# First query block of a sliding-window attention: no value product and no scores for the empty block in front of it

## The chip, the core and the metric

The kernel runs on one core of a Trainium2 chip. The metric is device time in microseconds (us) of one execution of the whole program, as the median of several runs. The profile is of one execution; its span goes from the first to the last instruction. The engines are named as the profile names them: PE for matmuls (TensorE), PEld for the loads of the stationary operand, DVE (VectorE), ACT (ScalarE), POOL (GpSimd), and SP for the queue that issues most transfers.

## The reference, cut to what matters

One inference step of a two-layer decoder, all in float32: a causal pooling mixer, then sliding-window attention with learned sinks. There are 1024 prompt positions and 8 single-token decode rows; the model width is 2048, with 32 query heads and 4 key/value heads of 64.

```
def banded_blocks(a):                       # each block of 128 keys with the block in front of it
    ax = jnp.concatenate([jnp.zeros_like(a[:, :WINDOW]), a], axis=1)
    ax = ax.reshape(B, nb + 1, WINDOW, *a.shape[2:])
    return jnp.concatenate([ax[:, :-1], ax[:, 1:]], axis=2)

s = jnp.einsum('...qkgd,...skd->...kgqs', q, k) * (HEAD_DIM ** -0.5)
mask = (kp <= qp) & (qp - kp < WINDOW) & (kp >= 0)
s = jnp.where(mask, s, NEG)
m = jnp.maximum(jnp.max(s, axis=-1, keepdims=True), sink)
p = jnp.exp(s - m)
p = p / (jnp.sum(p, axis=-1, keepdims=True) + jnp.exp(sink - m))
o = jnp.einsum('...kgqs,...skd->...qkgd', p, v)
```

Queries come in blocks of 128. Each block sees its own 128 keys and the 128 in front of them, of which the mask leaves the trailing 128 positions. The first block of the prompt has nothing in front of it: its front block is a block of zeros with positions below zero, and the mask (`kp >= 0`) leaves none of it.

## The kernel before

The prompt is worked on in two chunks: chunk c = 0 holds positions 0 to 511, chunk c = 1 positions 512 to 1023 and the decode rows. Each layer is an input projection and an output projection (`PHASES`: ai, ao for the first layer, bi, bo for the second), once per chunk. A projection in float32 precision is three matmuls for each piece of weights: high part by high part, high by low, low by high (L684 to L686 in the projections that use Strassen's seven products, L712 to L714 in the plain ones). The weights come by SP from memory, DVE adds or subtracts pieces of them (L349), ACT rounds them to the high part (L505), DVE forms the low part (L520).

The attention of a chunk is woven into its bi phases. It goes by 16 tiles t of two heads each; of a tile, head j sits on 64 of the 128 partitions. `attend(c, t, ...)` books the steps of one tile on later ticks of the projection: `product` puts a piece of PE work behind the weights of that tick, `at` a piece of other work. The steps of one tile, in order:

- `score` (L1878). For each of NB = 4 query blocks b, each head j and each quarter a of the block (32 queries, h = 32a), one float32 matmul with 64 rows of contraction and 32 columns of stationary operand. Its moving operand is the band of 160 keys that those 32 queries can see: from key h of the block in front to key h + 31 of the own block. Eight such matmuls (4 quarters, 2 heads) make a block, 32 a tile of heads. They write `self.S` (the program's pS) in PSUM, where a block has 256 columns: 128 for the front block's keys, 128 for its own.
- `select` and `largest` copy the front half out to SBUF with ACT (L1895) and put the own half over it with DVE where key <= query, so that 128 columns hold the whole window. In chunk 0 the front half of block 0 isn't read: POOL fills its place with -1e30 (L1893), and ACT copies blocks 1 to 3 alone.
- `expo`, `total` and `norm` (ACT, DVE) make the probabilities, `turn` (L1931, PE) transposes them, `keep` copies them to `w` (ACT) and, with those of own keys set to zero, to `wp` (DVE, L1941).
- `values` (L1955): for each block b, the own values times `w`, then the difference "front values minus own values" (`Vd`) times `wp`, added in PSUM; in each, head j is one float32 matmul with 128 rows and 64 columns of stationary operand and 128 moving columns. That is 4 matmuls a block, 16 a tile. In chunk 0, block 0, `wp` is all zeros, since no key of the front block has a probability.
- `gate` (L1964, DVE) multiplies with the gate, and the result goes to memory.

The keys lie in `kT` with 128 columns in front of the chunk's 512; in chunk 0 POOL sets these 128 to zero, in chunk 1 they are the last keys of chunk 0 (`kv_open`).

PE, DVE and ACT run in the order of the source: a function at the end of the build ties each instruction to the one before it on its engine. The instructions on SP and POOL are ordered by the scheduler of the language's library, which also sets all waits.

Of the kernel before, what the change touches and what calls it, by code (L numbers as in the profile page):

```python
# [16 lines left out]
P = 128  # L17
# [173 lines left out]
class Kern:  # L191
# [1670 lines left out]
    def attend(self, c, t, at, s1, s2, late=False, ticks=CLOSE):  # L1862
# [6 lines left out]
        x = {}  # L1869

        def score():
            s, q, lastq = self.qs.pop((c, t))
            for b in range(NB):
                for j in range(2):
                    r = slice(64 * j, 64 * j + 64)
                    for a in range(4):
                        h, k = 32 * a, b * P + 32 * a
                        nc.tensor.matmul(  # L1878
                            self.S[h : h + 32, j, b * 256 + h : b * 256 + h + 160], q[r, k : k + 32],
                            self.kT[t // 8][r, k : k + 160], start=True, stop=True,  # L1880
                        )
            if lastq:
                s.free()
# [63 lines left out]
        def values():  # L1947
            o = x["o"] = self.S[:, 1, :512] if late else self.psO()
            for b in range(NB):
                bs = slice(b * P, (b + 1) * P)  # L1950
                for n, (V, p) in enumerate(((self.V[b + 1], x["w"].a), (self.Vd[b], x["wp"].a))):
                    for j in range(2):
                        vs = slice((2 * (t // 8) + j) * HD, (2 * (t // 8) + j + 1) * HD)
                        ms = slice((2 * b + j) * P, (2 * b + j + 1) * P)
                        nc.tensor.matmul(  # L1955
                            o[64 * j : 64 * j + 64, bs], V[:, vs], p[:, ms], start=n == 0, stop=n == 1
                        )
            x["w"].free()
            x["wp"].free()

        def gate():
# [13 lines left out]
            if j == 1 or t == 15 or self.sg.get((c, t + 1), (None,))[0] is not z:  # L1975
                z.free()

        self.product(at, 2, score)
        for n, go in zip(ticks, (
            select, largest, lambda: expo(0), lambda: expo(1), total, lambda: norm(0), lambda: norm(1)  # L1980
        )):
            self.at(at + n, go)
        self.product(at + s1, 0, turn)
        self.at(at + s1 + 1, keep)
        self.product(at + s1 + s2, 1, values)
        self.at(at + s1 + s2 + 1, gate)

# [501 lines left out]
```

## Time and profile before

| | |
|---|---|
| runs | 2308.86, 2309.34 and 2309.92 us (median 2309.34) |
| span of the profiled execution | 2308.8 us, 50518 instructions; its own device time isn't listed apart from the span |
| granted TensorE clock | 0.999 over the span |
| scores (L1878) | 2048 records on PE in 32 places (16 tiles by 2 chunks), 64 x 32 stationary, 160 moving columns |
| values (L1955) | 1024 records on PE in 32 places, 128 x 64 stationary, 128 moving columns |
| those of chunk 0 | scores from 1148.1 to 1524.6 us, values from 1193.6 to 1558.6 us |

A matmul of two float32 operands leaves two records on PE and two on PEld, so a tile's 32 score matmuls are 64 records and its 16 value matmuls 32. Records overlap: a row's duration holds the time that the array takes to pass data through, and the pace at which work goes on is read from the starts of neighbouring records, not from durations. In a timeline, neighbouring records of one line are merged into one row with their count; a row of a very short stretch holds those that are open in it.

### The profile page before, as it was taken

Reading aid. Unit: us, or ns where it says so; the run is one execution under the profiler, and the core shown is the slowest. Engines: PE = TensorE matmul, PEld = TensorE weight load, DVE = VectorE, ACT = ScalarE, POOL = GpSimd, SP = SyncE. Lnnn points to the kernel's source line nnn. Section 1 sums busy time; section 2 is a strip of 40 time slices with the busy share of each in tenths; the row PEclk is TensorE's granted clock in tenths of the full one; section 3 lists DMA queues with packets and bytes.
Section 4 is the critical chain, followed back from the end, with each engine's and each line's share of the span. In section 5 each row is a group of like instructions: output and inputs, shape, how many; then the busy total and the mean of one; then the engine's idle time right before and its main releaser. Section 6 shows DMA issues by size and latency. Waiting matters only on the chain.

```text
span 2308.8 us, 50518 instructions
## 1 busy us (share of the span) xinstructions
PE 2286.2 (99%) x20417; PEld 2216.1 (96%) x20417; DVE 1943.5 (84%) x2415; ACT 1389.0 (60%) x2547; POOL 191.1 (8%) x359
## 2 busy tenths in 40 slices
PE   9999999999999999999999999999999999999998
PEld 7999999999999999999889999999999999999998
DVE  8888889877868878998878888999877777888997
ACT  5544446544546556555576766785776678656665
POOL 0111100010000000000001111100000000000001
PEclk9999999999999999999999999999999999999999
DMA  7879679988989989999767667777787778799894
GB/s 260 284 245 315 229 252 327 317 302 300 303 304 323 339 293 321 317 385 359 235 241 249 224 237 243 263 273 233 236 261 233 248 241 293 245 365 360 286 342 149
DMA packets 246395, 648.31 MB, mean 281 GB/s; under 512 B 25201, under 2 KB 106001, under 8 KB 246161
## 3 DMA queue, kind: packets, MB, share of 16 engines
q1 hardware_dynamic: 204288, 493.13, 63.7%
q0 software_dynamic: 41872, 151.96, 17.0%
q8 instruction: 159, 2.61, 0.5%
q14 instruction: 76, 0.61, 0.1%
HBM read 463.00 MB, written 172.47 MB: 275 GB/s over the span
## 4 chain that ended last, share of the span: by engine, by line
PE 56%; DVE 1%; DMA 1%; ACT 0%; issue 0%; POOL 0%; SPq 0%; DVEq 0%; POOLq 0%
PE pD L684 15%; PE pD L686 14%; PE pD L685 14%; PE pO L1955 2%; PE pD L712 2%; PE pD L714 2%; PE pD L713 2%; PE pS L1878 2%; PE pS L1931 1%; DMA m<-in_wob 0%; PE pS L1955 0%; PE pO L684 0%; PE pO L685 0%; PE pO L686 0%; DVE m L520 0%; DMA m<-in_wib 0%
## 5 line engine op out<-in xcount | busy, mean ns | idle before, releaser
L684 PE MATMUL pD<-m,m 128*128 128x260 f32 (+1 forms) x5088 | 1441.1, 283 | 4.4 <-ACT pD L623 2.2
L686 PE MATMUL pD<-m,m 128*128 128x260 f32 (+1 forms) x5088 | 1434.0, 282 | 5.8 <-DVE m L520 5.8
L685 PE MATMUL pD<-m,m 128*128 128x260 f32 (+1 forms) x5088 | 1434.2, 282 | 0.0
L684 PEld LDWEIGHTS pD<-m,m 128*128 128x128 f32 x5088 | 958.9, 188 | 13.7 <-issue 6.2
L686 PEld LDWEIGHTS pD<-m,m 128*128 128x128 f32 x5088 | 959.5, 189 | 7.6 <-DVE m L520 7.4
L685 PEld LDWEIGHTS pD<-m,m 128*128 128x128 f32 x5088 | 958.6, 188 | 0.5
L520 DVE TENSOR_TENSOR m<-m,m 128x1024 fp32r<-128x1024 f32 x690 | 834.1, 1219 | 94.4 <-ACT m L505 37.9
L505 ACT CAST m<-m 128x1024 fp32r<-128x1024 f32 x690 | 720.6, 1049 | 247.5 <-DVE m L349 122.4
L349 DVE TENSOR_TENSOR m<-m,m 128x1024 f32<-128x1024 f32 x136 | 166.2, 1222 | 8.6 <-DMA m<-in_wia 5.6
L847 DVE TENSOR_TENSOR m<-m,m 128x1024 fp32r<-128x1024 f32 (+1 forms) x118 | 144.0, 1225 | 7.4 <-ACT m L838 5.8
L838 ACT CAST m<-m 128x1024 fp32r<-128x1024 f32 (+1 forms) x118 | 123.3, 1051 | 8.3 <-DVE m L520 3.9
L657 ACT COPY m<-pD 128x260 f32<-128x260 f32 (+1 forms) x88 | 32.9, 374 | 125.8 <-PE pD L686 125.6
L645 DVE TENSOR_TENSOR m<-pD,m 128x260 f32<-128x260 f32 (+1 forms) x92 | 38.3, 417 | 74.3 <-ACT pD L644 68.2
L1914 ACT ACTIVATE m<-m,sm 128x128 f32<-128x128 f32 x256 | 99.4, 392 | 0.0
L623 ACT ACTIVATE pD<-pD 128x260 f32<-128x260 f32 (+1 forms) x90 | 33.3, 370 | 98.8 <-PE pD L686 98.4
L1181 PE MATMUL pD<-m,m 128*128 128x260 f32 (+1 forms) x528 | 91.5, 323 | 0.0
L712 PE MATMUL pD<-m,m 128*128 128x512 f32 x224 | 89.1, 398 | 0.0
L714 PE MATMUL pD<-m,m 128*128 128x512 f32 x224 | 88.2, 394 | 0.0
L713 PE MATMUL pD<-m,m 128*128 128x512 f32 x224 | 88.1, 393 | 0.0
L1181 PEld LDWEIGHTS pD<-m,m 128*128 128x128 f32 x528 | 79.4, 188 | 8.2
L1927 ACT ACTIVATE m<-m,sm 128x128 f32<-128x128 f32 x256 | 81.9, 391 | 7.8 <-DVE sm L1922 7.2
L632 ACT COPY m<-pD 128x260 f32<-128x260 f32 (+1 forms) x92 | 34.4, 374 | 82.6 <-PE pD L686 82.4
(257 smaller groups left out, 2102.7 us busy)
## 6 DMA issues: line engine op xcount, KB each, us to landing
m<-in_wib SPq DMA_DIRECT2D x132, 512.0 KB
m<-in_wia SPq DMA_DIRECT2D x128, 512.0 KB
m<-swoa SPq DMA_DIRECT2D x64, 512.0 KB
swia<-m POOLq DMA_DIRECT2D x56, 512.0 KB, 4.8
m<-swia SPq DMA_DIRECT2D x56, 512.0 KB
m<-swob SPq DMA_DIRECT2D x56, 512.0 KB
m<-in_wob SPq DMA_DIRECT2D x52, 512.0 KB
m<-in_woa SPq DMA_DIRECT2D x48, 512.0 KB
```

The costliest lines, as they stand in the source:

```text
L349: self.nc.vector.tensor_add(s[out].a[:, :1024], s[x].a[:, :1024], s[y].a[:, :1024])
L505: self.nc.scalar.copy(hi.r[:, :1024], self.stream[self.cast].src().a[:, :1024])
L520: self.nc.vector.tensor_sub(lo.r[:, :1024], s.src().a[:, :1024], hi.a[:, :1024])
L684: nc.tensor.matmul(ps[:, :TH], wh[:, s], h, start=new and k == 0, stop=False, skip_group_check=on)
L685: nc.tensor.matmul(ps[:, :TH], wh[:, s], l, start=False, stop=False, skip_group_check=on)
L686: nc.tensor.matmul(ps[:, :TH], wl[:, s], h, start=False, stop=k == 7, skip_group_check=on)
L712: nc.tensor.matmul(ps[:], wh[:, s], h, start=par == 0 and k == 0, stop=False)
L713: nc.tensor.matmul(ps[:], wh[:, s], l, start=False, stop=False)
L714: nc.tensor.matmul(ps[:], wl[:, s], h, start=False, stop=par == 1 and k == 7)
L838: self.nc.scalar.copy(h.r[:, :n], s.a[:, :n])
L847: self.nc.vector.tensor_sub(l.r[:, :n], s.a[:, :n], h.a[:, :n])
L1181: nc.tensor.matmul(ps[:, : cs.stop - cs.start], ws[:, s], d[:, cs], start=f0 and k == 0, stop=l0 and k == 3,)
```

## The change

In chunk 0, block 0 alone, and for each of the 16 tiles of heads:

- the score matmul of quarter h begins at its own block's first key: `f = P - h` columns are left out in front. The moving widths become 32, 64, 96 and 128 instead of 160 each. The number of matmuls stays.
- the product of `Vd[0]` with `wp` is left out: two matmuls less, and the product with the own values opens and closes the accumulation.

The columns of `S` that are no longer written are those that `select` doesn't read. Nothing else in the source changes.

```
                         h, k = 32 * a, b * P + 32 * a
+                        f = P - h if c == 0 and b == 0 else 0
                         nc.tensor.matmul(
-                            self.S[h : h + 32, j, b * 256 + h : b * 256 + h + 160], q[r, k : k + 32],
-                            self.kT[t // 8][r, k : k + 160], start=True, stop=True,
+                            self.S[h : h + 32, j, b * 256 + h + f : b * 256 + h + 160], q[r, k : k + 32],
+                            self.kT[t // 8][r, k + f : k + 160], start=True, stop=True,
                         )
...
-                for n, (V, p) in enumerate(((self.V[b + 1], x["w"].a), (self.Vd[b], x["wp"].a))):
+                parts = [(self.V[b + 1], x["w"].a), (self.Vd[b], x["wp"].a)][: 1 if c == 0 and b == 0 else 2]
+                for n, (V, p) in enumerate(parts):
...
-                            o[64 * j : 64 * j + 64, bs], V[:, vs], p[:, ms], start=n == 0, stop=n == 1
+                            o[64 * j : 64 * j + 64, bs], V[:, vs], p[:, ms], start=n == 0, stop=n == len(parts) - 1
```

On PE, the scores of the first tile of chunk 0 (m_1542 holds the keys, m_1599 the queries), before:

```order
L714 MATMUL pD_13611<-m_1509_12863,m_1601_13533 128x512
L1878 MATMUL pS_13088<-m_1542_13089,m_1599_13529 32x160 x32
L712 MATMUL pD_13611<-m_1516_12904,m_1602_13535 128x512
```

and now:

```order
L714 MATMUL pD_13611<-m_1509_12863,m_1601_13533 128x512
L1879 MATMUL pS_13088<-m_1542_13089,m_1599_13529 32x32
L1879 MATMUL pS_13088<-m_1542_13089,m_1599_13529 32x64
L1879 MATMUL pS_13088<-m_1542_13089,m_1599_13529 32x96
L1879 MATMUL pS_13088<-m_1542_13089,m_1599_13529 32x128
L1879 MATMUL pS_13088<-m_1542_13089,m_1599_13529 32x32
L1879 MATMUL pS_13088<-m_1542_13089,m_1599_13529 32x64
L1879 MATMUL pS_13088<-m_1542_13089,m_1599_13529 32x96
L1879 MATMUL pS_13088<-m_1542_13089,m_1599_13529 32x128
L1879 MATMUL pS_13088<-m_1542_13089,m_1599_13529 32x160 x24
L712 MATMUL pD_13611<-m_1516_12904,m_1602_13535 128x512
```

The first eight of the 32 are narrower; their place between the projection's matmuls is the same.

On PE, the values of the same tile (m_1662 is `w`, m_1663 `wp`, m_1544 the own values, m_1545 the differences), before:

```order
L1955 MATMUL pO_14133<-m_1662_14103,m_1544_13091 64x128 x2
L1955 MATMUL pO_14133<-m_1663_14104,m_1545_13092 64x128 x2
L1955 MATMUL pO_14133<-m_1662_14103,m_1544_13091 64x128 x2
L1955 MATMUL pO_14133<-m_1663_14104,m_1545_13092 64x128 x2
L1955 MATMUL pO_14133<-m_1662_14103,m_1544_13091 64x128 x2
L1955 MATMUL pO_14133<-m_1663_14104,m_1545_13092 64x128 x2
L1955 MATMUL pO_14133<-m_1662_14103,m_1544_13091 64x128 x2
L1955 MATMUL pO_14133<-m_1663_14104,m_1545_13092 64x128 x2
```

and now:

```order
L1957 MATMUL pO_14133<-m_1662_14103,m_1544_13091 64x128 x4
L1957 MATMUL pO_14133<-m_1663_14104,m_1545_13092 64x128 x2
L1957 MATMUL pO_14133<-m_1662_14103,m_1544_13091 64x128 x2
L1957 MATMUL pO_14133<-m_1663_14104,m_1545_13092 64x128 x2
L1957 MATMUL pO_14133<-m_1662_14103,m_1544_13091 64x128 x2
L1957 MATMUL pO_14133<-m_1663_14104,m_1545_13092 64x128 x2
```

The first pair on `wp` and the differences is gone, and the two products on own values of blocks 0 and 1 follow each other.

On SP, early in chunk 0, with the waits that each transfer has, before:

```order
L285 DMA m33_1748_15038<-in_wib 128x1024 [waits DMAHW0_49,DMASW1_49,DVE_49]
L285 DMA m39_1738_14880<-in_wib 128x1024 [waits DMAHW1_49,PE_49,Activation_49]
L285 DMA m41_1751_15079<-in_wib 128x1024 [waits DMAHW2_49,DVE_49,Activation_49]
L285 DMA m0_1756_15122<-in_wib 128x1024 [waits DMAHW3_49,DMASW0_49,PE_49]
L285 DMA m5_1755_15120<-in_wib 128x1024 [waits DMAHW4_49,PE_49]
```

and now:

```order
L285 DMA m33_1748_15030<-in_wib 128x1024 [waits DMAHW0_49,DMASW1_49,DVE_49]
L285 DMA m39_1738_14874<-in_wib 128x1024 [waits DMAHW1_49,PE_49,Activation_49]
L285 DMA m41_1751_15071<-in_wib 128x1024 [waits DMAHW2_49,DVE_49,Activation_49]
L285 DMA m5_1755_15112<-in_wib 128x1024 [waits DMAHW3_49,DMASW0_49,PE_49]
L285 DMA m0_1756_15114<-in_wib 128x1024 [waits DMAHW4_49,DMASW0_49]
```

Two loads of weights that stand next to each other (into the buffers m0 and m5) have changed places. The other rows of SP, and all of DVE, ACT and POOL, are the same operations on the same buffers in the same order. One wait is gone as well: the first score of chunk 0 waited for DVE and POOL (which had set the front keys to zero) and now waits for DVE alone.

## The prediction

> **What bounds the kernel now.** I read the page's busy times first, then PE's waits in the stretch that is changed, then the chain of waits.
>
> ```profile
> PE 2286.2 (99%) x20417; PEld 2216.1 (96%) x20417; DVE 1943.5 (84%) x2415; ACT 1389.0 (60%) x2547; POOL 191.1 (8%) x359
> ```
>
> PE is busy for 99% of the span. Records overlap, so this says that PE hardly ever stands still, not that it is at its peak. The two stretches "from just before the first score of chunk 0 to its last values" and "all that follows" (length, then busy time of PE, PEld, DVE, ACT, POOL; clock; share of the DMA engines):
>
> ```profile
> core 0: us, PE busy (x) PEld busy (x) DVE busy (x) ACT busy (x) POOL busy (x), PEclk, DMA share, GB/s
> 1146.00:1559.00 413.00, 412.54 (x4291) 390.00 (x4291) 361.58 (x436) 295.83 (x680) 46.39 (x93) 1.00 0.72 249
> 1559.00:2308.80 749.80, 735.31 (x7275) 721.61 (x7271) 622.96 (x779) 489.61 (x985) 48.91 (x80) 1.00 0.79 269
> ```
>
> In the changed stretch PE stands still for 0.46 of 413 us, at the full clock; DVE is at 88%, ACT at 72%, the DMA engines at 72%. So PE sets the pace there and the others have room for a PE that is 1% faster. What PE waited for, from 1140 to 1575 us:
>
> ```profile
> PE pD L672 <- ACT m L657: 0.5, 1, 0.5
> PE pD L686 <- DVE m L520: 0.2, 1, 0.2
> ```
>
> The first is one ACT copy between two matmuls, and it moves with PE. The second lies behind the last values, and the chain of waits shows what it hangs on:
>
> ```profile
> 1558.59 0.13 PE pD L686
> 1558.72 0.23 SPq L285
> ...
> 1559.05 6.82 DMA m<-in_wib
> ...
> 1569.78 1.14 DVE m L520
> ...
> 1570.97 0.39 PE pD L686
> ```
>
> A projection's matmul ends, that frees a buffer, SP issues a load, DVE works on it, and PE takes it up at 1570.97: 12.25 us from PE to PE. The values of the last tile lie inside this loop (they begin at 1558.6).
>
> **The scores.** First the cost of a score block as it is. The timeline of PE around the first one:
>
> ```profile
> 1147.81 0.40 PE L714 MATMUL pD<-m,m 128*128 128x512 f32 x1
> 1148.13 1.32 PE L1878 MATMUL pS<-m,m 64*32 64x160 f32 x64
> 1149.38 0.50 PE L712 MATMUL pD<-m,m 128*128 128x512 f32 x1
> ```
>
> 64 records of about 0.3 us each take 1.25 us from first start to the next matmul's start, so many run side by side. How many, short stretches show (the number behind PE's busy time counts the records open in a stretch):
>
> ```profile
> 1148.13:1148.19 0.06, 0.06 (x8) 0.06 (x13) 1.00 0.72 274
> 1148.19:1148.29 0.10, 0.10 (x8) 0.10 (x16) 1.00 0.78 258
> 1148.29:1148.35 0.06, 0.06 (x16) 0.06 (x12) 1.00 1.21 343
> ```
>
> Eight start within 0.06 us, none in the next 0.10, then eight more: bursts of eight, one for each of the block's eight places on the array (2 heads by 4 quarters). A block has 16 records, two bursts; a tile has eight bursts. Their pace, from two moments at which just two bursts are open (the row begins with the older one):
>
> ```profile
> 1148.43 0.48 PE L1878 MATMUL pS<-m,m 64*32 64x160 f32 x16
> 1148.97 0.48 PE L1878 MATMUL pS<-m,m 64*32 64x160 f32 x16
> ```
>
> These are bursts 3 and 7: 0.54 us for four, 0.136 a burst (0.1358 from the unrounded starts). What sets it? The values go in pairs (two heads) of 128 moving columns. Two moments nine pairs apart, and the whole block:
>
> ```profile
> 1193.77 0.50 PE L1955 MATMUL pO<-m,m 128*64 128x128 f32 x6
> 1194.75 0.50 PE L1955 MATMUL pO<-m,m 128*64 128x128 f32 x6
> 1193.61 1.97 PE L1955 MATMUL pO<-m,m 128*64 128x128 f32 x32
> ```
>
> 0.98 us for nine, 0.109 a pair. 0.136 to 0.109 is 1.25, and 160 to 128 columns is 1.25: both blocks go by the columns that one place passes, 0.85 ns a column and record, however many places work beside it. So in block 0 each burst is over when its widest quarter is: 128 columns, 0.109 us. The quarters of 32, 64 and 96 columns end earlier and their places then wait for the others or run ahead, but the fourth quarter's place still has 2 x 128 + 6 x 160 columns to pass. Saved: 2 x (0.136 - 0.109) = 0.054 us a tile, 16 x 0.054 = 0.87 us. The change takes half of the block's columns away, and a fifth of its time.
>
> Bounds: if unequal quarters kept the old rhythm, 0. If columns counted by their sum, half of two bursts, 0.136 us a tile or 2.18 us. I take 0.87, since the proportion to the width is measured on both kinds.
>
> **The values.** Two matmuls less are four records, two pairs: 2 x 0.109 = 0.218 us a tile, 3.50 us for 16. A second way to price them is by share of the block; the chain of waits gives the time on the path for a score block, a value block, and a value block of the decode rows with 8 moving columns:
>
> ```profile
> 1148.21 1.25 PE pS L1878 x64
> 1193.68 1.90 PE pO L1955 x32
> 1795.84 1.03 PE pO L2089 x32
> ```
>
> 1.90 x 4/32 = 0.238 us, 3.80 us in all. That counts a part of the block's entry and exit as if it shrank with the block. The decode row shows that it doesn't: 32 records of next to no columns still cost 1.03 us, at most 0.064 a pair, which is also the floor under narrow matmuls and lies below the 0.109 that I use. I take 3.50, with 3.80 as the upper end. The Trainium skill, TensorEngine Tiling (Array Packing), Key Properties, says the same of the ends of a block: changing the tiling mode drains the array. By that rule entry and exit stay and the sum is 3.50; by share it would be 3.80.
>
> **What is lost on the way.** The last tile's 0.22 us lies inside the loop from 1558.72 to 1570.97, which does not shrink: PE arrives earlier and waits 0.4 us in place of 0.2. The other tiles' savings lie ahead of that loop's start. Behind it, the larger waits hang on transfers that PE itself releases:
>
> ```profile
> 1927.35 0.13 PE pD L686
> 1927.48 0.32 SPq L828
> 1927.85 10.07 DMA m<-in_wob
> ...
> 2078.85 0.14 PE pD L686
> 2079.01 5.92 DMA m<-o
> ```
>
> In both the issue follows a PE matmul at once. PE's waits at their ends, the two largest behind 1575 us (1945.4 and 2087.3 us), are
>
> ```profile
> PE pD L686 <- DVE m L520: 2.5, 1, 2.5
> PE pD L684 <- ACT m L657: 1.7, 1, 1.7
> ```
>
> These loops begin earlier by what PE gained and keep their length. I count nothing for them.
>
> **The swapped loads** cost nothing: both end in the same DVE subtraction, and behind it there is slack.
>
> ```profile
> 1275.02 1.89 SPq L285 DMA_DIRECT2D m<-in_wib  x4
> 1280.51 1.22 DVE L349 TENSOR_TENSOR m<-m,m 128x1024 f32<-128x1024 f32 x1 [0.51 <-DMA m<-in_wib]
> 1286.92 2.35 DVE L520 TENSOR_TENSOR m<-m,m 128x1024 fp32r<-128x1024 f32 x2
> 1292.30 0.28 PE L686 MATMUL pD<-m,m 128*128 128x256 f32 x1
> ```
>
> The pair is issued at 1275.0 and 1275.4, the subtraction at 1280.51 reads both, the first DVE result of it is ready at about 1288.1 and PE takes it at 1292.30. Were one landing later, the first 4.2 us would be free, and what goes beyond them PE would wait. The POOL wait that the first score loses was for this, 82 us before that score starts, so it held nothing up:
>
> ```profile
> 1066.28 0.21 POOL L1753 MEMSET m<- 128x128 f32 x1 [1.79 <-DVE m L520]
> ```
>
> **Sum.** 3.50 + 0.87 - 0.22 = 4.15 us. Against the span 2308.8 that is 2304.6. The median of the runs lies 0.5 us above the span, so I predict 2309.34 - 4.15 = 2305.2 us, 0.18% faster. About 0.2%, 4.6 us, is what a measurement of this kernel can tell from no change: the forecast lies just inside it. Its bounds: scores worth nothing, 3.28 us gained, 2306.1; the block priced by share, 4.45 us, 2304.9.
>
> **Rivals.**
>
> *Narrow counts in full.* The early quarters' places run ahead into the next blocks and every column saved is time saved: 2.18 + 3.50 - 0.22 = 5.46 us, 2303.9. For it: the places hold their own weights, and within a tile nothing makes one wait for another by the code. Against it: the fourth quarter's places have no more than 2 x 32 columns less, and the block ends with them.
>
> *The gain is eaten behind the stretch.* If the transfers at 1927 or 2079 hung on a full queue and not on PE, the waits behind them (1.7 and 2.5 us) would grow by what PE gained: between 2305.2 and 2309.3, with half of it 2307.3. Against it: the chain, which puts a PE matmul directly in front of each issue. For it: that many loads share the same queue, and the order of landings can shift a little when PE is 4 us early.
>
> *Unequal widths break the bursts.* No row of this trace has matmuls of different widths side by side. If the array took the first eight of each tile one after another, 16 records of 80 columns on average at 0.85 ns would cost 1.09 us in place of 0.27, 0.82 more a tile, 13.1 us in all, less 3.28 from the values: 2319.2 us, slower. It would have to cost over 0.49 us a tile, (3.28 + 4.6)/16, to come out as slower. Against it: even equal matmuls are issued 0.007 us apart and each goes on in its own place. The Trainium skill, TensorEngine Tiling (Array Packing), Key Properties, holds that tiles operate independently; by that rule this rival falls away, but no run here shows it for unequal widths.
>
> **Chances.** Forecast 0.60, narrow in full 0.20, eaten 0.15, broken bursts 0.05. Of the forecast's share I put a sixth, 0.10, beyond 4.6 us: its bound by share, 4.45, is close, and the three runs alone differ by 1.06 us. That makes faster by over 0.2% 0.20 + 0.10 = 0.30, within it 0.50 + 0.15 = 0.65, slower 0.05. The range for 8 in 10 goes from 2303.2 (narrow in full, with half a microsecond of spread) to 2307.6 (half eaten); what it leaves out is the broken bursts and the worse half of "eaten".
>
> **What would show it.** PE has 20353 records, 64 less. In chunk 0, bursts 1 to 3 of a score block start 0.109 apart and the later ones 0.136, and the block takes 1.19 us on the chain in place of 1.25; with narrow in full it would be 1.11, with broken bursts about 2. A value block takes 1.68 us in place of 1.90. The stretch from the first score to the last values is 4 us shorter, and the wait behind the last values grows from 0.2 to 0.4 us. From there to the end every piece keeps its length and starts 4.15 us earlier; if instead a wait near 1945 or 2087 has grown by that much, the gain was eaten. I am wrong if a score block of chunk 0 takes other than 1.19 us, or if the shift at 1575 us is not the shift at the end.

## The result, and the profile after

The changed kernel takes 2303.96 us (median of 11 runs, 2302.37 to 2307.35), the kernel before 2309.32 (11 runs beside them, 2306.61 to 2312.13). The ratio is 0.9978, with a 95% interval from 0.9970 to 0.9987: 5.4 us less, between 3.0 and 6.9. The forecast was 4.15 us less, 2305.2, in a range from 2303.2 to 2307.6.

The profiled execution of the changed kernel has a span of 2305.6 us and took 2307.35 us in all, so its own time lies 1.8 us above its span. It was the slowest of the 11, so its span is not the place to read the gain; its parts are. The page's busy times:

```profile
PE 2281.9 (99%) x20353; PEld 2211.4 (96%) x20353; DVE 1942.7 (84%) x2415; ACT 1388.5 (60%) x2547; POOL 192.3 (8%) x359
```

PE has 64 records less, 20353. The first score block of chunk 0 and the first value block, on the timeline and on the chain of waits:

```profile
1152.69 1.26 PE L1879 MATMUL pS<-m,m 64*32 64x32 f32 x64
1153.88 0.50 PE L712 MATMUL pD<-m,m 128*128 128x512 f32 x1
...
1152.76 1.19 PE pS L1879 x52
1198.13 1.68 PE pO L1957 x28
```

1.19 us a score block in place of 1.25, 1.68 us a value block in place of 1.90: both as forecast. From here on I call "the stretch" the time from the first score of chunk 0 to the first score of chunk 1, and read it from these two starts. Before (first two rows) and after (last two):

```profile
1148.13 0.76 PE L1878 MATMUL pS<-m,m 64*32 64x160 f32 x29
1596.86 0.91 PE L1878 MATMUL pS<-m,m 64*32 64x160 f32 x40
```

```profile
1152.69 0.81 PE L1879 MATMUL pS<-m,m 64*32 64x32 f32 x39
1597.09 0.90 PE L1879 MATMUL pS<-m,m 64*32 64x160 f32 x39
```

448.73 us before, 444.40 after: 4.32 us shorter from the unrounded starts. By the blocks it would be 4.35: the median score block of chunk 0 takes 1.2475 us before and 1.194 after, the median value block 1.8975 and 1.679, and there are 16 of each. PE's waits from 1140 to 1575 us are the same 0.5 and 0.2 us as before. The first score, however, starts 4.6 us later in this execution. What PE waited for from 900 to 1140 us, where both programs hold the same instructions, is after:

```profile
PE pD L684 <- ACT pD L644: 2.3, 1, 2.3
PE pD L686 <- DVE m L520: 1.6, 2, 1.4
PE pO L952 <- DVE m L936: 0.3, 1, 0.3
```

and before it was 0.5 us in all. Behind the stretch the changed kernel needs 708.5 us, the kernel before 711.9. So the two spans differ by +4.6 ahead, -4.3 in the stretch and -3.4 behind, 3.2 us less in sum. Only the middle term lies where the programs differ. The experiments ask three things: whether the stretch is explained by the two terms of the sum, what the rest of the time does by itself, and why a part of the gain is sometimes missing in the stretch.

### The profile page after: what moved, and what is told of

It reads as the page before. It is cut to its first block, busy times and chain, and to the rows that moved or that the text cites. A ratio compares the mean times of both kernels' runs of the same rounds, so it can differ in the third digit from the quotient of the medians.

```text
span 2305.6 us, 50389 instructions
## 1 busy us (share of the span) xinstructions
PE 2281.9 (99%) x20353; PEld 2211.4 (96%) x20353; DVE 1942.7 (84%) x2415; ACT 1388.5 (60%) x2547; POOL 192.3 (8%) x359
## 3 DMA queue, kind: packets, MB, share of 16 engines
q8 instruction: 159, 2.61, 0.5%
## 4 chain that ended last, share of the span: by engine, by line
PE 54%; DVE 2%; DMA 2%; ACT 1%; issue 1%; SPq 0%; POOL 0%; DVEq 0%; POOLq 0%; ACTq 0%
PE pD L684 14%; PE pD L686 13%; PE pD L685 13%; PE pD L712 2%; PE pO L1957 2%; PE pD L714 2%; PE pD L713 2%; PE pS L1879 2%; PE pS L1932 1%; DMA m<-in_woa 1%; DVE m L520 1%; DMA h<-m 0%; DMA m<-swob 0%; PE pS L1957 0%; PE pO L684 0%
## 5 line engine op out<-in xcount | busy, mean ns | idle before, releaser
L520 DVE TENSOR_TENSOR m<-m,m 128x1024 fp32r<-128x1024 f32 x690 | 833.4, 1218 | 93.4 <-ACT m L505 37.9
L657 ACT COPY m<-pD 128x260 f32<-128x260 f32 (+1 forms) x88 | 32.9, 374 | 118.2 <-PE pD L686 117.9
```

What stands on the lines that cost most here:

```text
L520: self.nc.vector.tensor_sub(lo.r[:, :1024], s.src().a[:, :1024], hi.a[:, :1024])
```

## The experiments

Of each kernel the table gives the stretch and what lies behind it, read from its profile as above, and the median of its runs where it was timed several times against the kernel before (2309.0 to 2309.1 us, 21 to 25 runs). Four kernels ran once each and have no time here. All cuts of code show the difference from the changed kernel; "..." stands for what is left out of a line. Where only one half is on trial, the other is set back as in the first two cuts.

| kernel | stretch | against 448.7 | behind | time | ratio (95%) |
|---|---|---|---|---|---|
| before | 448.72 | | 711.9 | 2309.32 | |
| before again | 448.72 | 0.00 | 708.0 | | |
| after | 444.40 | -4.32 | 708.5 | 2303.96 | 0.9978 (0.9970 to 0.9987) |
| after again | 445.61 | -3.11 | 708.0 | 2303.51 | 0.9979 (0.9970 to 0.9989) |
| values only | 446.11 | -2.61 | 708.6 | 2304.58 | 0.9980 (0.9971 to 0.9989) |
| scores only | 447.92 | -0.81 | 708.8 | 2308.62 | 0.9997 (0.9988 to 1.0006) |
| first three quarters trimmed | 448.69 | -0.03 | 710.0 | | |
| fourth quarter trimmed | 448.74 | +0.02 | 709.2 | | |
| last tile only | 448.50 | -0.22 | 710.2 | | |
| value product left out in four blocks | 437.72 | -11.00 | 710.8 | 2296.84 | 0.9946 (0.9932 to 0.9959) |
| product twice | 452.23 | +3.51 | 708.6 | 2311.03 | 1.0009 (1.0000 to 1.0018) |
| tile 10 earlier | 444.33 | -4.39 | 709.8 | 2305.67 | 0.9984 (0.9976 to 0.9993) |

### The two halves

The value half alone:

```
-                        f = P - h if c == 0 and b == 0 else 0
+                        f = 0
```

> The value product of the empty block is left out, the scores stay 160 wide. Result as the reference's. Theory (pairs of records at 0.109 us, two pairs less a tile, nothing lost behind): from the first score of chunk 0 to the first score of chunk 1, 448.8 us before, the stretch is 3.50 us shorter, and a value block of chunk 0 takes 1.68 us on the chain in place of 1.90. By share of the block it would be 3.80 us. Rival (eaten behind the stretch): the stretch shrinks by 3.5 but the time by less than 2. Time by the theory: 3.5 us less than before, plus or minus the 1 us or so by which medians of a few runs differ.

The score half alone:

```
-                parts = [(self.V[b + 1], x["w"].a), (self.Vd[b], x["wp"].a)][: 1 if c == 0 and b == 0 else 2]
+                parts = [(self.V[b + 1], x["w"].a), (self.Vd[b], x["wp"].a)][:2]
```

> The scores of chunk 0, block 0, are narrowed to the own keys, and the value product stays. Result as the reference's. Theory (the block ends with its widest quarter): a score block of chunk 0 takes 1.19 us on the chain in place of 1.25, the stretch from the first score of chunk 0 to that of chunk 1 is 0.87 us shorter, the time 0.9 us less, which is within 0.2%. Rival (columns count by their sum): 1.11 us and 2.18 us. Rival (only the whole change together gives more than its parts): with the values alone the two don't add up to the stretch of the change, which was 4.32 us shorter.

The scores: 1.19 us a block (first start 1148.91, next matmul 1150.11), a stretch 0.81 us shorter, a time that can't be told from no change. That is the widest quarter's price (0.87) and not the columns' (2.18).

The values: the median value block of chunk 0 goes from 1.898 to 1.679 us, 0.219 less, which is 3.50 us for 16. The two halves add up to the change block by block. Yet the stretch is only 2.61 us shorter. PE's waits in it (1140 to 1600 us):

```profile
PE pO L1957 <- DVE m L1942: 0.6, 1, 0.6
PE pD L672 <- ACT m L657: 0.5, 1, 0.5
PE pD L686 <- DVE m L520: 0.2, 1, 0.2
```

The last two are there before as well. The first is new: the values of tile 10 stop in the middle for `wp`, and their block takes 2.50 us in place of 1.68. That is 0.82 of the missing 0.89 us. It was not in the forecast, and the section on tile 10 takes it up.

### Which columns count

The first three quarters trimmed (32, 64, 96 columns), the fourth left at 160:

```
-                        f = P - h if c == 0 and b == 0 else 0
+                        f = P - h if c == 0 and b == 0 and a < 3 else 0
```

> In chunk 0, block 0, the scores of the first three quarters are narrowed (32, 64, 96 columns), the fourth keeps 160; the value product stays. 9/10 of the columns that the change takes from the scores are gone. Result as the reference's. Theory (the widest place decides): a score block stays at 1.25 us on the chain, the stretch from the first score of chunk 0 to that of chunk 1 is no shorter than 448.8, within 0.1 us. Rival (columns by their sum): 1.96 us shorter. Rival (the early quarters give part of it by running ahead): in between.

And only the fourth trimmed:

```
-                        f = P - h if c == 0 and b == 0 else 0
+                        f = P - h if c == 0 and b == 0 and a == 3 else 0
```

> In chunk 0, block 0, only the fourth quarter's scores are narrowed, from 160 to 128 columns; the other three keep 160; the value product stays. Result as the reference's. Theory (the widest place decides): nothing, 1.25 us a block, although with the other three trimmed as well it gave 0.054 us a block. Rival (it is the fourth quarter alone, as the last in order, that counts): 1.19 us a block and 0.87 us off the stretch. Rival (sum of columns): 0.22 us off the stretch.

The first score block with three quarters trimmed:

```profile
1148.72 1.32 PE L1879 MATMUL pS<-m,m 64*32 64x32 f32 x64
1149.97 0.50 PE L712 MATMUL pD<-m,m 128*128 128x512 f32 x1
```

and with the fourth trimmed:

```profile
1148.60 1.32 PE L1879 MATMUL pS<-m,m 64*32 64x160 f32 x64
1149.85 0.50 PE L712 MATMUL pD<-m,m 128*128 128x512 f32 x1
```

1.25 us both times, as before, and the stretches are unchanged to 0.03 us. Nine tenths of the columns are worth nothing, the last tenth alone is worth nothing, and together they give 0.05 us a block. Both rivals on the scores are out: neither the sum of the columns nor the last quarter in order decides, but the place that has most to pass.

### The last tile

```
-                ...[: 1 if c == 0 and b == 0 else 2]
+                ...[: 1 if c == 0 and b == 0 and t == 15 else 2]
```

> Only the last tile of chunk 0 (t = 15) loses the value product of the empty block; all else as before. Result as the reference's. The prediction counted this tile's 0.22 us as lost in the loop from 1558.72 to 1570.97 us. If that holds, the stretch from the start of that value block to the first score of chunk 1 is as long as before (38.2 us) and the wait of PE at its end grows from 0.2 to 0.4 us. Theory now: DVE waits at 1564.4 for a matmul that stands behind those values, so the loop hangs on the values as well, and the stretch is 0.22 us shorter with the wait unchanged at 0.2.

From the start of that value block to the first score of chunk 1 it is 38.00 us in place of 38.22, and the wait at the end stays at 0.2 us. So this tile's 0.22 us is not lost. The rows that show why stood in the timeline of DVE before:

```profile
1564.44 0.43 DVE L895 TENSOR_TENSOR m<-m 128x256 f32<-128x256 f32 x1 [0.86 <-PE pD L685]
1564.79 0.42 DVE L896 TENSOR_TENSOR m<-m 128x256 f32<-128x256 f32 x1
1565.12 0.42 DVE L897 TENSOR_TENSOR m<-m,m 128x256 f32<-128x256 f32 x1
1565.57 0.43 DVE L898 TENSOR_TENSOR m<-m,m 128x256 f32<-128x256 f32 x1
```

The chain of waits said that the load's landing at 1565.87 released DVE's work at 1565.92. But the work released at 1565.92 stands behind these four instructions, and the first of them had waited for a PE matmul that ended at 1564.4, behind the values. That work starts 0.34 us after the start of the last of the four here, and also 0.34 us after it in the second profile of before, in the changed kernel's first and in this one, where no landing lies just ahead of it. So the landing held nothing up; it only happened to come last.

### The same program again

> The kernel before, profiled once more. Theory (waits on transfers outside the stretch differ from execution to execution): the stretch from the first score of chunk 0 to that of chunk 1 is 448.8 us within 0.1, while the start of that first score, 1148.1 us, or the time behind the stretch, 711.9 us, differs by more than 0.5 us from the first profile. Rival (the program repeats itself, and the 4.5 us that the changed kernel lost ahead of the stretch came from the change): both are the same within 0.3 us.

The stretch is the same to the hundredth. Behind it the kernel before takes 708.0 us this time and 711.9 the first time. Its PE waits from 1900 to 2120 us were, in the first profile

```profile
PE pD L686 <- DVE m L520: 2.5, 1, 2.5
PE pD L684 <- ACT m L657: 1.7, 1, 1.7
PE pS L1878 <- DVE m L1848: 0.4, 1, 0.4
```

and in the second

```profile
PE pD L684 <- ACT m L657: 1.4, 1, 1.4
PE pD L686 <- DVE m L520: 0.6, 1, 0.6
PE pS L1878 <- DVE m L1848: 0.2, 1, 0.2
```

4.6 and 2.2 us. The first profile has something else behind its longest wait:

```profile
2087.00:2090.00 3.00, 2.67 (x12) 2.67 (x13) 2.91 (x4) 1.72 (x4) 0.53 (x1) 0.50 1.04 404
```

```profile
2087.91 0.21 PE pD L684
2088.12 0.21 PE pD L685
...
2090.44 0.12 PE pD L684
2090.56 0.12 PE pD L685
```

From 2087 to 2090 us the granted clock (third number from the end) was 0.50, and PE's matmuls followed each other at 0.21 us in place of 0.12. That cost 1.3 us more. In the other eleven profiles the clock is whole from 20 to 2290 us, also behind a wait of 2.3 us (changed kernel, 1012 us) and of 2.0 us (tile 10 earlier, 2083 us); why it fell here stays open. The rest of the program does not keep its length from one execution to the next. That explains a term of about 4 us behind the stretch in a comparison of two single profiles; the 4.6 us ahead of it didn't show again in any other profile (the first score starts between 1148.0 and 1149.3 us in the other eleven).

The changed kernel again, unchanged:

> The changed kernel once more, beside the two halves on one chip. Theory (the stretch carries the whole gain, the rest of the difference is where waits on transfers fall in one execution): the stretch from the first score of chunk 0 to that of chunk 1 is again 4.3 us shorter than 448.8, whatever the time ahead of it is, and the time is 4.3 us below before, between 3.3 and 5.3. Rival (the swapped loads or something else gives another microsecond): the time is again 5 to 6 us below, and the excess lies in the same place of the profile.

2303.51 us, 5.6 us below before; the first comparison had 5.4. So by the medians the time is a microsecond or more beyond the sum, the rival's 5 to 6. The theory missed on both counts, since the stretch is only 3.11 us shorter here. The waits of PE in it (1140 to 1600 us) say where 1.2 us went:

```profile
PE pD L672 <- ACT m L657: 1.0, 1, 1.0
PE pO L1957 <- DVE m L1942: 0.4, 1, 0.4
PE pD L686 <- DVE m L520: 0.2, 1, 0.2
```

The value block of tile 10 takes 2.33 us in place of 1.68, 0.66 more. The first wait has grown by 0.55. In the first profile of before ACT stood idle for 0.45 us ahead of that copy (L657), so it had time to spare; here it had waited 1.86 us for DVE (L520) at 1497.35 and came to the copy without a pause.

Nor does the excess lie behind the stretch: the 708.0 us there, with three waits of 2.0 us in sum, are what the kernel before needed in its second profile. Part of it lies outside the span, in what the device time has beyond it. In all 20 runs of the changed kernel that is 1.7 to 1.8 us; in the 25 and 21 runs of before in the two later comparisons it is 1.7 to 3.0, in the mean 2.3 and 2.1. It is 1.7 to 1.8 in the other kernels too whose value products were changed in 16 tiles, the one with the product twice among them, and 1.8 to 3.0 with the scores alone. Why stays open. What is left is in the scatter: the spans of the nine runs here are 4.2 us below before in the mean and 5.1 in the median, since two of the nine lie 3 to 4 us above that median. The sum of 4.37 us fits the mean.

### Four times as much, and the opposite

The product with the differences left out in all four blocks of chunk 0; the front keys' part of the output is missing there:

```
-                ...[: 1 if c == 0 and b == 0 else 2]
+                ...[: 1 if c == 0 else 2]
```

> All four blocks of chunk 0 lose the product of the differences with the front part of the probabilities (so the front keys' share of the output is wrong in blocks 1 to 3: left out); scores stay. Four times the value half of the change. Theory: 8 pairs less a tile, 16 x 8 x 0.109 = 14.0 us off the stretch and off the time, 0.6%. Rival (eaten behind the stretch by waits on transfers): the stretch shrinks by 14.0 but the time by clearly less, under 10 us. By share of the block, 15.2.

A value block takes 1.02 us (1193.49 to 1194.52), 0.874 less, four times 0.219: the price holds. But the stretch loses 11.0 and not 14.0 us. Of the missing 3 us, PE's waits in the stretch hold most:

```profile
PE pS L1879 <- DVE m L1942: 2.0, 2, 1.3
PE pD L672 <- ACT m L657: 0.8, 1, 0.8
PE pD L686 <- DVE m L520: 0.4, 2, 0.2
```

With so much less to do at the values, PE meets the next score while DVE is still reading the same PSUM for `wp`, at tiles 8 and 10. The time is 12.3 us less: it lies between the theory and the rival, and the waits that can be seen lie in the stretch and not behind it.

The opposite, the product with zeros added twice in block 0:

```
+                if c == 0 and b == 0:
+                    parts.append(parts[1])
```

> The opposite of the value half: in chunk 0, block 0 the product of the differences with the front part of the probabilities, which is all zeros there, is added twice; scores as before. Result as the reference's. Theory (a pair of records costs 0.109 us wherever PE has no slack): a value block of chunk 0 takes 2.12 us on the chain in place of 1.90, the stretch from the first score of chunk 0 to that of chunk 1 is 3.50 us longer than 448.7, since a later PE gives DVE more room at the values of tile 10, and the time is 3.5 us more than before, 2 to 5. Rival (what lies behind the stretch gets shorter when PE comes to it earlier, and longer when later): the time is 4.5 us more or over, and the waits of PE at 1936, 1945 and 2087 us, shifted, are larger than the 2.0 to 4.6 us of the two profiles of before.

The value block takes 2.12 us, the stretch is 3.51 us longer, with no wait at tile 10: the theory to the hundredth. The time is 2.0 us more, at the lower end of what I expected and 1.5 us short of the stretch; about 0.3 of that is the smaller part outside the span, the rest stays open. The rival had 4.5 or more. Its waits at 1941, 1949 and 2090 us are 0.6, 0.9 and 1.3, in sum 2.7. So coming later made them no larger. The rival, by which the part behind the stretch gets shorter when PE comes earlier, falls.

### Tile 10

In the kernel with the value half alone, at the values of tile 10, on DVE and on PE:

```profile
1442.00 2.36 DVE L520 TENSOR_TENSOR m<-m,m 128x1024 fp32r<-128x1024 f32 x2 [3.22 <-DMA to<-m]
...
1450.08 1.22 DVE L1942 TENSOR_TENSOR m<-pS,cst 128x1024 f32<-128x1024 f32 x1
```

```profile
1450.09 0.66 PE L1957 MATMUL pO<-m,m 128*64 128x128 f32 x8
1451.35 0.88 PE L1957 MATMUL pO<-m,m 128*64 128x128 f32 x12 [0.60 <-DVE m L1942]
```

DVE stood still for 3.2 us until a store (to<-m) had landed, and then had seven instructions to do ahead of `wp`. PE began with the products on `w`, ran eight records and waited: without the first product on `wp`, the ninth record is the first that reads it. Before, the same place:

```profile
1442.31 2.36 DVE L520 TENSOR_TENSOR m<-m,m 128x1024 fp32r<-128x1024 f32 x2 [2.10 <-DMA to<-m]
...
1450.39 1.22 DVE L1941 TENSOR_TENSOR m<-pS,cst 128x1024 f32<-128x1024 f32 x1
```

`wp` was done at 1451.60, the values began at 1451.76, and their fifth record, the first that reads `wp`, at 1452.03: 0.43 us to spare, 1.22 in the second profile of before. PE had gained 2.2 us by tile 10 (ten tiles by 0.219), of which 1.7 show on the profile's clock, as this execution came to the stretch 0.5 us later. DVE, which hung on a store, came only 0.3 us earlier: `wp` was done at 1451.30, 0.7 us after the ninth record could have begun. In the first profile of the changed kernel it was done 0.13 us ahead of that record, and there was no wait. To test it, the transposes and copies of tile 10 alone were put one tick earlier:

```
+                s1, s2 = (11, 3) if (c, t) == (0, 10) else (s1, 2)
-                self.attend(c, t, at, s1, 2, t > 12, ticks)
+                self.attend(c, t, at, s1, s2, t > 12, ticks)
```

> The changed kernel, and for tile 10 of chunk 0 alone the transposes of the probabilities and the copies behind them (w on ACT, wp on DVE) stand one tick earlier, with the values where they were. Result as the reference's. In three kernels with the value half PE waited 0.4 to 1.3 us at the values of tile 10 for wp, since DVE had just waited 2 to 3 us for a store. Theory (that wait is what the stretch lost): no wait of PE at those values, the stretch is 4.3 us shorter than 448.7 (4.37 less the wait of 0.46 at 1506 if that has grown), and the time is 0 to 1 us below the changed kernel's 2303.5 to 2304.0. Rival (DVE is late as a whole there, and the wait turns up at the next thing that PE takes from it): the stretch is again 2.6 to 3.2 us shorter, with a wait elsewhere. As buffers are handed out in another order from there on, waits on transfers behind the stretch may differ.

```profile
1443.11 1.23 DVE L1942 TENSOR_TENSOR m<-pS,cst 128x1024 f32<-128x1024 f32 x1 [0.98 <-ACT m L1941]
...
1450.08 1.75 PE L1957 MATMUL pO<-m,m 128*64 128x128 f32 x28
```

`wp` is now ready 5.7 us ahead, the values run through, and the stretch is 4.39 us shorter, the whole sum of 4.37. The theory on the stretch holds. The time does not follow: 2305.67 us, 2 us more than the changed kernel. Its profile has a wait of 2.0 us at 2083 us, where the changed kernel had 0.6 and 0.4. From tile 10 on the buffers are handed out in another order, so I can't say that the earlier transposes and nothing else did that. It beats the kernel before, not the change. The expectation speaks of three kernels that waited there for `wp`; it was two. With all four blocks left out, nothing of chunk 0 reads `wp`, and the waits of 1.3 us at tile 8 and 0.7 at tile 10 were those of the next scores.

## Why the prediction was right, and where it was not

**What bounds the kernel.** PE in the stretch: right. That "the others have room for a PE that is 1% faster" is wrong for DVE at one place. DVE's 88% is an average; at tile 10 it had 0.4 and 1.2 us to spare behind a store, and in two of three profiles of kernels with the value half and the old order (after again, values only) the value block there took 0.66 and 0.82 us longer. That the wait for the ACT copy "moves with PE" holds only as long as ACT has time to spare: in after again it grew from 0.46 to 1.01 us. I had read PE's waits, and a wait that isn't there yet has no row; the spare time of the producer ahead of each consumer would have shown it.

**The scores**, 0.87 us: measured 0.0535 us a block, 0.86 for 16, and 0.81 on the stretch. The reason given, that a block ends with its widest place, is shown by the two trimmed kernels. The picture of bursts, the first three 0.109 us apart, is wrong; behind the first eight starts there are no bursts any more (below).

**The values**, 3.50 us: measured 0.2185 us a block, 3.50 for 16, four times it in four blocks, and the same with the other sign. The price by share of the block, 3.80, is out.

**The last tile's loss**, 0.22 us: wrong. The loop from 1558.72 to 1570.97 was one by the chain of waits alone. The landing that it named held nothing up, and the wait at its end stayed at 0.2 us.

**The swapped loads**, nothing: right. PE has no new wait from 1140 to 1575 us in the first profile after.

**What lies behind**: "keep their length" is the step that failed. The prediction named a sign of being wrong, a shift at 1575 us that is not the shift at the end, and this sign is there: in the first profile after, PE comes out of the wait at 1571 us 0.2 us later than before and the end 3.2 us earlier. But the kernel before does the same to itself, 0.1 us later and 3.8 us earlier in its second profile. Its three waits add up to 4.6 and 2.2 us, those of the changed kernel to 2.7 and 2.0, and the first profile of before has the 1.3 us at half clock besides. So the sign can't be read from two single profiles.

**The time.** 2305.2 was forecast, 0.18% and just inside 0.2%; it came to 2303.96, 0.22% and just outside, with an interval on both sides of the bound, and inside the range. It is also, within 0.1 us, the 2303.9 of "narrow in full", which the score blocks rule out: the time alone would have named the wrong cause. The sum of 4.15 us (4.37 without the last tile's term) lies inside the interval of the measurement, 3.0 to 6.9; of the microsecond by which the medians go beyond it, 0.3 to 0.5 lie outside the span, and the rest is not told from scatter. The step from span to median was also wrong: the median was said to lie 0.5 us above the span, since the first profile's own time wasn't known. In the later runs of before the time lies 1.7 to 3.0 us above the span and the median span is 2306.8 to 2307.0, so the profiled execution with its 2308.8 was about 2 us longer than usual. The forecast starts from the median of the runs, so this did not reach it.

**The rivals.** Narrow in full: out, by the scores alone and both trimmed kernels. Broken bursts: out, 1.19 us a block, with unequal widths side by side. Eaten behind the stretch: not seen; what can be seen to be eaten was eaten inside it.

## What to carry to other kernels

Where several small matmuls run side by side in places of the array, as the scores do here, only the place with the most columns sets the block's time: trim all of the widest ones or none. A gain on the bounding engine has to be checked against each producer that it waits for, by the time between the producer's end and the consumer's start, since the tightest one takes the first share. When parts of a program vary by microseconds between executions, measure a small change over the stretch that it touches, and profile the kernel before twice.

## What the runs showed of the hardware

Places of the array run ahead of each other, out of the matmuls' order in the program. In the changed kernel, with widths of 32 to 128 columns in block 0 and 160 from block 1 on, the records on PE open between 1152.78 and 1152.80 us, about 0.1 us into the block, are by shape:

```profile
L1879 PE MATMUL pS<-m,m 64*32 64x128 f32 x2 | 0.3, 293 | 0.0
L1879 PE MATMUL pS<-m,m 64*32 64x160 f32 x1 | 0.3, 299 | 0.0
L1879 PE MATMUL pS<-m,m 64*32 64x64 f32 x3 | 0.3, 232 | 0.0
L1879 PE MATMUL pS<-m,m 64*32 64x96 f32 x2 | 0.3, 267 | 0.0
L1879 PE MATMUL pS<-m,m 64*32 64x32 f32 x4 | 0.3, 203 | 0.0
```

Block 0 has four records of each width. A matmul of block 1 (160 columns) has started, while of each of block 0's matmuls at 96 and at 128 columns only the first record has: their second records start 0.12 to 0.18 us into the block, the one of block 1 at 0.08. The rows don't name the places; it fits that a place that was done with its 32 columns took the next block's work. The eight-fold bursts of the kernel before were no rule of the array but the look of eight equal widths.
